# Grouping by array mode in a scan of two linear-attention mixers: sums on 64 rows into two PSUM banks, neighbours by sums over features

## The chip, the cores and the metric

The kernel runs on one core of a Trainium2 chip. The metric is the device time in microseconds (us) of one launch. The engines are PE (matrix products), DVE, ACT and POOL (elementwise work, each with its own in-order queue) and SP, which here only issues transfers.

## The reference

One layer of a backbone over 2048 latent tokens and 256 context tokens, of width 1024. After a modulated RMSNorm, one dense projection makes the inputs of two bidirectional linear-attention mixers of four heads each. The first, GLA, has a decay for each of 64 key features; the second, Gated DeltaNet (GDN below), has a short convolution, one decay per head and delta rules. Both scan over chunks forward and backward, and start the latent tokens from the context's final state. In GLA one chunk needs decayed scores, an output and a new state:

```python
bc = jnp.cumsum(gc, axis=3)
diff = bi[:, :, :, None, :] - bi[:, :, None, :, :]
dec = jnp.exp(jnp.where(causal[:, :, None], diff, -jnp.inf))
att = jnp.einsum('bhtd,bhsd,bhtsd->bhts', qi, ki, dec)
o = jnp.einsum('bhtd,bhde->bhte', qi * jnp.exp(bi), s) + jnp.einsum('bhts,bhse->bhte', att, vi)
s_new = s * jnp.exp(bl[:, :, 0, :])[..., None] + jnp.einsum('bhsd,bhse->bhde', ki * jnp.exp(bl - bi), vi)
```

The outputs of both directions are added, normalised per head, gated, projected (`w_gla_out`, `w_gdn_out`), merged by sigmoid gates, projected by `w_o` and added to the input, which a last RMSNorm normalises.

## The kernel before

It has three phases. `phase_proj` (to about 1375 us) makes all inputs in dense products and stores them in device memory; `phase_mix` (to about 1820) runs the scans; `phase_out` runs the output products. Chunks are of 128 tokens: 2 of context and 16 latent.

`phase_mix` is a loop of 17 steps, `si`. Step `si` prepares the chunk `si` of the forward direction and the chunk `15 - si` of the backward one (`gla_load`, `gla_step`) and, at the same time, scans the pair that the step before prepared (`gdn_scan` and `gla_scan`, one of each per direction). Each is a Python generator; `weave` takes a piece of each in turn, by weights, and a scheduler in the build then fixes one order for each engine. From there every queue is in order: an instruction that waits holds up all behind it.

Scores of GLA within a chunk are built by levels, `LEVELS = (64, 32, 16, 8, 4, 2, 1)`: at level m, the later block of each pair of blocks of m tokens looks at the earlier one. Per group of two levels (`gla_group`, three groups), PE sums the log decays over tokens, for 128 features at a time (`ct`) and both directions, in products with a table of zeros and ones, `wt` (L1110: 128 rows, 256 columns, type fp32r, the decays split into a high part `gh` and a low part `gl`). ACT takes the exponentials out of PSUM (L1192, L1195), DVE multiplies them by q (L1201) and POOL by k (L1202). `gla_lev` then makes one level's scores: four heads of 64 features, hence four products on 64 rows of PE (L1226), into one of two slots of the PSUM tile `lv`. A slot is copied into the scores `at` by ACT for m = 64 (two copies, L1230) or, with a mask, by DVE (L1233). Level 1, the neighbours, needs only each token's own decay: transposes (L1213), exponentials (L1215), a product with q (L1216), then `gla_lev` like the others.

`gla_ends` makes the decays to the chunk's ends (L1110, L1119), `gla_kt` and `gla_qe` the decayed keys and queries. `gla_scan` updates the state (L1282, products with 64 columns) and makes the outputs: scores times values (L1306, 128 rows), the queries times the state (L1310, 64 rows), written to `oi` by ACT (L1314) or, when the other direction's output `prev` exists, added to it by DVE (L1316). `gdn_scan` has blocks of four products with 128 rows at L1042, L1053, L1063, L1072 and L1082; its output is complete at L1083. A product in f32 is two passes on PE, so that a block of four shows as x8 in the trace.

For the first eight scanned pairs the outputs are only stored (`put_o`). After that each chunk's output meets the stored one of its other direction, loaded by `prev_o`, and goes through `finish`, four times a step: four squares on ACT with a sum (L1344), Ln and Exp on ACT (L1345, L1346), a normalisation on POOL (L1347), four transposes on PE (L1352), a gating product on DVE (L1354), with a load of the gates and a store of the result. The squares and their sums go to tiles with two buffers, so that a third finish waits for the normalisation of the first. I call these steps the second half of the mix, the others the first half. `finish` runs woven into the end of its step.

"Array mode" below is the shape of the part of PE that a product uses: 128 rows by 128 columns, 64 rows by 128 columns, 128 rows by 64 columns.

## Time and profile before

| | |
|---|---|
| time before, median of 3 runs | 2199.81 us (2198.74 to 2201.21) |
| the profiled execution: its time | 2198.7 us |
| its span | 2196.9 us |
| mean granted clock of PE | 0.989 |
| DMA traffic | 315.68 MB, 142 GB/s over the span |

A profile page gives the busy time of each engine, then the span in slices, DMA queues, the chain of work that ended last, and the costliest groups of instructions. A row of a timeline holds the start, the duration, the engine, the line of the kernel, the operation with output and inputs, the part of PE in use (rows*columns), the shape, the number of instructions joined in the row and, in brackets, the idle time of the engine just before and who ended it. A row of groups holds the sum of busy time, the mean in ns, and the idle time before. On PE durations overlap, since products are pipelined: the pace is the distance between starts.

### The profile page before, as it was taken

Reading aid. Unit: us, or ns where it says so; the run is one execution under the profiler, and the core shown is the slowest. Engines: PE = TensorE matmul, PEld = TensorE weight load, DVE = VectorE, ACT = ScalarE, POOL = GpSimd, SP = SyncE. Lnnn points to the kernel's source line nnn. Section 1 sums busy time; section 2 is a strip of 40 time slices with the busy share of each in tenths; the row PEclk is TensorE's granted clock in tenths of the full one; section 3 lists DMA queues with packets and bytes.
Section 4 is the critical chain, followed back from the end, with each engine's and each line's share of the span. In section 5 each row is a group of like instructions: output and inputs, shape, how many; then the busy total and the mean of one; then the engine's idle time right before and its main releaser. Section 6 shows DMA issues by size and latency. Waiting matters only on the chain. (4 is left out here: it accounts for less than half of the span.)

```text
span 2196.9 us, 40078 instructions
## 1 busy us (share of the span) xinstructions
PE 2122.3 (97%) x15168; PEld 1764.3 (80%) x15168; DVE 1245.2 (57%) x2178; ACT 884.2 (40%) x2188; POOL 858.2 (39%) x765
## 2 busy tenths in 40 slices
PE   5999999999999999999999998999999988999998
PEld 2688888888888888777777776888878877999888
DVE  3813555567776554655555554666777776444333
ACT  3654255455542223443434443444544444111211
POOL 2410122222320115665666662555555554322331
PEclk8999999999999999999999999999999999999999
DMA  8323122222222234443444435888688858433322
GB/s 281 104 89 115 53 60 68 63 63 61 70 75 74 83 89 137 140 141 116 134 150 145 146 134 174 281 303 277 227 267 287 263 176 254 138 120 125 101 80 84
DMA packets 275005, 315.68 MB, mean 144 GB/s; under 512 B 22280, under 2 KB 206716, under 8 KB 274812
## 3 DMA queue, kind: packets, MB, share of 16 engines
q1 hardware_dynamic: 274812, 313.12, 44.4%
q8 instruction: 120, 1.97, 0.4%
q14 instruction: 73, 0.60, 0.1%
HBM read 203.20 MB, written 109.84 MB: 142 GB/s over the span
## 5 line engine op out<-in xcount | busy, mean ns | idle before, releaser
L365 PE MATMUL pz<-hi,wh 128*128 128x512 f32 (+1 forms) x1560 | 621.3, 399 | 1.7 <-DVE hi L133 1.7
L365 PE MATMUL pz<-lo,wh 128*128 128x512 f32 (+1 forms) x1560 | 600.3, 385 | 1.8 <-POOL lo L134 1.8
L365 PE MATMUL pz<-hi,wl 128*128 128x512 f32 (+1 forms) x1520 | 588.0, 387 | 0.0
L365 PEld LDWEIGHTS pz<-lo,wh 128*128 128x128 f32 x1560 | 294.5, 189 | 51.0 <-POOL lo L134 3.6
L365 PEld LDWEIGHTS pz<-hi,wh 128*128 128x128 f32 x1560 | 294.2, 189 | 48.0 <-DVE hi L133 2.5
L365 PEld LDWEIGHTS pz<-hi,wl 128*128 128x128 f32 x1520 | 286.2, 188 | 53.7 <-issue 0.4
L134 POOL TENSOR_TENSOR wl<-w,wh 128x1024 fp32r<-128x1024 f32 x44 | 110.6, 2514 | 436.2 <-ACT wh L131 311.9
L563 DVE SCALAR_TENSOR_TENSOR acc<-zpad,cw,acc 128x1024 f32<-128x1024 f32 x192 | 268.2, 1397 | 6.7
L1519 PE MATMUL pm<-yh,wab 128*128 128x256 f32 x1024 | 187.9, 284 | 4.4 <-DVE mt L1523 4.4
L867 DVE CAST_PREDICATED U<-kit,pl 128x256 f16<-128x256 int32 x216 | 91.3, 432 | 138.7 <-PE pl L990 134.9
L1519 PEld LDWEIGHTS pm<-yh,wab 128*128 128x128 f32 x1024 | 161.3, 193 | 5.1 <-ACT wo L131 4.7
L1588 PE MATMUL pz<-wo,mh 128*128 128x512 f32 (+1 forms) x528 | 161.2, 388 | 0.0
L1519 PE MATMUL pm<-yl,wab 128*128 128x256 f32 x512 | 145.7, 285 | 0.8 <-POOL yl L134 0.8
L983 ACT CAST ppb<-pl 128x256 f16<-128x256 f32 x216 | 73.6, 374 | 166.4 <-PE pl L982 160.0
L1588 PEld LDWEIGHTS pz<-wo,mh 128*128 128x128 f32 x528 | 98.4, 189 | 20.2
L134 DVE TENSOR_TENSOR sql<-sq,sqh 128x512 fp32r<-128x512 f32 (+1 forms) x36 | 28.0, 805 | 141.6 <-ACT sqh L131 141.4
L618 POOL TENSOR_TENSOR acc<-acc,sq 128x512 f32<-128x512 f32 x32 | 50.2, 1576 | 138.4 <-ACT sq L617 78.6
L1588 PE MATMUL pz<-wo,ml 128*128 128x512 f32 (+1 forms) x264 | 101.8, 386 | 0.0
L1519 PEld LDWEIGHTS pm<-yl,wab 128*128 128x128 f32 x512 | 98.7, 193 | 1.7 <-POOL yl L134 1.2
L1202 POOL TENSOR_TENSOR E<-E,ak 128x256 f32<-128x256 f32 x96 | 76.8, 820 | 58.9 <-ACT E L1192 44.7
L134 POOL TENSOR_TENSOR yl<-wr,yh 128x1024 fp32r<-128x1024 f32 x16 | 40.3, 2542 | 134.2 <-ACT yh L131 134.2
L1233 DVE COPY_PREDICATED at<-am,lv 128x512 f32<-128x512 int32 x96 | 70.5, 734 | 31.5 <-PE lv L1226 29.4
(292 smaller groups left out, 4190.5 us busy)
## 6 DMA issues: line engine op xcount, KB each, us to landing
dgate<-ob SPq DMA_DIRECT2D x96, 256.0 KB
gd<-dgd SPq DMA_DIRECT2D x32, 768.0 KB
w<-in_w_in SPq DMA_DIRECT2D x44, 512.0 KB
qk<-dqkv SPq DMA_DIRECT2D x32, 512.0 KB
ga<-dgate SPq DMA_DIRECT2D x64, 256.0 KB
dqkv<-acc SPq DMA_DIRECT2D x192, 64.0 KB
dgd<-tm SPq DMA_DIRECT2D x36, 256.0 KB
dgd<-n SPq DMA_DIRECT2D x36, 256.0 KB
```

Source lines behind the costliest of these rows:

```text
L134: getattr(nc, lo).tensor_tensor(dst_lo, src, dst_hi.bitcast(F32), op=ALU.subtract)
L365: nc.tensor.matmul(ps[:, 0:n], a[:, kk, :], b[:, kk, :], start=(k == 0), stop=(k == last - 1))
L563: nc.vector.scalar_tensor_tensor(acc, src, wcol, acc, op0=ALU.mult, op1=ALU.add)
L618: nc.gpsimd.tensor_tensor(v, v, r, op=ALU.mult)
L867: self.nc.vector.copy_predicated(out, mv, data)
L983: nc.scalar.copy(ppl, pc.rearrange("p h (j i) -> p h j i", i=m))
L1202: nc.gpsimd.tensor_tensor(E[:, :, li, 1], E[:, :, li, 1], k, op=ALU.mult)
L1233: nc.vector.copy_predicated(at, self.am[:, i].unsqueeze(1).unsqueeze(1).broadcast_to([P, 2, 2, P]), ps)
L1519: nc.tensor.matmul(ps[:, half * 256:half * 256 + 256], wab[wi][:, k, j * P:(j + 1) * P], yy[:, k, :], start=(i == 0), stop=(i == 11))
L1588: nc.tensor.matmul(ps, aa[:, k, i * P:(i + 1) * P], wo[k][wi][:, cs], start=(j == 0), stop=(j == 23))
```

## The change

1. The table for the levels holds, for each half of a chunk's tokens, only that half's 64 columns (`WL` falls from 1024 to 640 columns a direction), since no level reaches over the middle of a chunk. A sum over tokens is made per half `x`: 64 rows of PE, 128 columns, into one PSUM bank for each half. A group has 16 such products, in pairs of the two halves, where it had 8 of full height. The exponentials are taken by half, eight a group.
2. Level 1 no longer goes through `gla_lev`. DVE makes decay times q of each token's neighbour, POOL multiplies by k (`gla_ones`), and two products with a two-column matrix `bones` sum over each head's 64 features (`gla_near`); a masked copy puts them into `at`.
3. `gla_lev` takes two levels at once: eight products on 64 rows, one after another, into both slots, and then the copies.
4. GLA's scan loses its own generator. `gla_state` makes both directions' new states in one block of 64-column products; `gla_out` makes both directions' outputs, the 64-row products last, right ahead of the first `gla_lev`. Both are called from the next pair's `gla_step`. The outputs of both directions go to one tile `og`, with one buffer, and the stored ones come in one tile `prevg`. The tiles `oi` and `prev` have two buffers where they had four.
5. The last step leaves out both mixers' state updates (`end`, `gla_end`).

The core of the diff. Lines that go are in the functions printed above.

```diff
-WL = 8 * P
+WL = 2 * P + 6 * 64
...
+            for x in range(2):
+                u = np.arange(64 * x, 64 * x + 64)
+                u = np.concatenate([u[np.isin(u, q)], u[~np.isin(u, q)]])
+                lev[i, 64 * x:64 * x + 64] = w[2 + i][64 * x:64 * x + 64][:, u]
+        cols = np.concatenate([*w[:2], *lev], 1)
...
-    def gdn_scan(self, r, need_o):
+    def gdn_scan(self, r, need_o, end=False):
...
-            oi = self.op.tile(B4, F32, name="oi", bufs=4)
+            oi = self.op.tile(B4, F32, name="oi")
...
+        if not end:
...
     def gla_group(self, r, i0):
...
+        E = self.gE.tile([P, 2, 2, 2, 2, 64], F32, name="E", bufs=3)
+        kl = self.gq.tile([P, 2, 2, P], F32, name="kl", bufs=3)
+        cols = slice(2 * P + i0 * 64, 2 * P + (i0 + 2) * 64)
+        ps = [self.pe().rearrange("p (l b c n) -> p l b c n", l=2, b=4, c=2) for _ in range(2)]
         for ct in range(2):
+            for d in range(2):
+                for j, g in enumerate(r["gg"]):
+                    for x in range(2):
+                        rows = slice(64 * x, 64 * x + 64)
+                        out = ps[x][:, :, 1:3, ct] if d == 0 else ps[x][:, :, 0:4:3, ct]
+                        nc.tensor.matmul(out, g[rows, d, ct * P:(ct + 1) * P], self.wt[rows, d, cols],
+                                         start=(j == 0), stop=(j == 1))
         for li in range(2):
+            m = LEVELS[i0 + li]
+            for x in range(2):
+                for qk in range(2):
+                    o = E[:, li, qk, x]
+                    if m == 64:
+                        i = ps[x][:, li, 1:3] if x != qk else ps[x][:, li, 0:4:3]
+                        i, o = i.rearrange("p a c n -> p c a n"), o.rearrange("p c (a n) -> p c a n", a=2)
+                    else:
+                        i = ps[x][:, li, 2 * qk:2 * qk + 2].rearrange("p e c (j i) -> p e (c j) i", i=m)
+                        o = o.rearrange("p c (j e i) -> p e (c j) i", e=2, i=m)
+                    nc.scalar.activation(o, i, AF.Exp, scale=1.0 / 16)
+        yield
+        for li in range(2):
+            nc.vector.tensor_tensor(E[:, li, 0], E[:, li, 0], byx(q), op=ALU.mult)
+            nc.gpsimd.tensor_tensor(byx(kl[:, li]), E[:, li, 1], byx(k), op=ALU.mult)
+        yield
+        return [(at, kl[:, li], E[:, li, 0], LEVELS[i0 + li]) for li in range(2)]
...
     def gla_ones(self, r):
...
+        w = self.gq.tile([P, 2, P], F32, name="qk1", bufs=1)
...
+        for d in range(2):
+            nc.vector.tensor_tensor(w[:, :, d:P:2], E[:, :, 1 - d:P:2], q[:, :, 1 - d:P:2], op=ALU.mult)
+        nc.gpsimd.tensor_tensor(w, w, k, op=ALU.mult)
+        return w
+    def gla_near(self, at, w):
+        nc = self.nc
+        pd = self.pe()
         for ct in range(2):
+            nc.tensor.matmul(pd[:, 2 * ct:2 * ct + 2], w[:, ct], self.bones, start=True, stop=True)
+        B = [P, 4, P]
+        nc.vector.copy_predicated(at, self.am[:, len(LEVELS) - 2].unsqueeze(1).broadcast_to(B),
+                                  pd[:, 0:4].unsqueeze(2).broadcast_to(B))
+    def gla_lev(self, levs):
+        nc, got = self.nc, []
+        for at, ks, ql, m in levs:
+            ps = self.slot()
+            for ct in range(2):
+                for hp in range(2):
+                    rows = slice(64 * hp, 64 * hp + 64)
+                    nc.tensor.matmul(ps[:, hp, ct], ks[rows, ct], ql[rows, :, ct], start=True, stop=True)
+            got.append((self.byhalf(at), ps, m))
+        for at, ps, m in got:
+            if m == 64:
+                for x in range(2):
+                    rows, cols = slice(64 * x, 64 * x + 64), slice(64 - 64 * x, 128 - 64 * x)
+                    nc.scalar.copy(at[rows, :, :, cols], ps[rows, :, :, cols])
+            else:
+                i = LEVELS.index(m) - 1
+                nc.vector.copy_predicated(at, self.am[:, i].unsqueeze(1).unsqueeze(1).broadcast_to([P, 2, 2, P]), ps)
+    def gla_step(self, f, b, prev):
...
+        if prev is not None:
+            S = self.gla_state(prev)
+            yield
+        levs = yield from self.gla_group(f, 0)
...
+        more = yield from self.gla_group(f, 2)
...
+        if prev is not None:
+            done = self.gla_out(prev, S)
+        self.gla_lev(levs)
+        if prev is not None:
+            done()
+            yield
+            yield from self.gla_put(prev)
+        yield
+        last = yield from self.gla_group(f, 4)
+        yield
+        self.gla_lev(more)
...
+        w = self.gla_ones(f)
...
+        yield
+        self.gla_lev(last)
+        yield
+        self.gla_near(f["at"], w)
+        yield
+    def gla_state(self, pair):
...
+        for d, r in enumerate(pair):
+            for h in range(4):
+                ct, hp = h // 2, h % 2
+                nc.tensor.matmul(ps[64 * hp:64 * hp + 64, (2 * d + ct) * P:(2 * d + ct + 1) * P],
+                                 r["kt"][:, 64 * h:64 * h + 64], r["v"][:, h * P:(h + 1) * P], start=True, stop=True)
...
+    def gla_out(self, pair, S):
...
+        po = [self.pv().rearrange("p (d c t) -> p d c t", d=2, c=2) for _ in range(2)]
...
+            nc.tensor.matmul(po[h % 2][:, 0, h // 2], f["at"][:, h], f["v"][:, h * P:(h + 1) * P],
+                             start=h < 2, stop=False, skip_group_check=True)
+        for d, r in enumerate(pair):
             for h in range(4):
...
+                nc.tensor.matmul(po[h % 2][:, d, ct], r["qe"][rows, ct], S[d][rows, ct], start=False,
+                                 stop=d == 1 and h >= 2, skip_group_check=True)
+        def done():
+            o = self.og = self.op.tile([P, 2, 4, P], F32, name="og", bufs=1)
+            v = lambda t, hp: t.rearrange("p d (c h) t -> p h d c t", h=2)[:, hp]
+            for hp in range(2):
+                if f["prev"] is None:
+                    nc.scalar.copy(v(o, hp), po[hp])
...
+                    nc.vector.tensor_tensor(v(o, hp), v(f["prev"], hp), po[hp], op=ALU.add)
+        return done
+    def gla_put(self, pair):
+        for d, r in enumerate(pair):
+            yield from self.put_o(0, r["c"] - NCTX, self.og[:, d])
...
+        t = pair[0]["prev"] = self.op.tile([P, 2, 4, P], F32, name="prevg", bufs=1)
+        for d, l in enumerate(ls):
+            self.nc.sync.dma_start(self.flat(t[:, d]), self.d_o[0][l])
...
+        t = self.op.tile([P, 4, P], F32, name="prev")
...
+                pair = [x[0] for x in prev]
+                self.gla_prev(pair)
+                for x in prev:
+                    x[1]["prev"] = self.prev_o(1, x[1]["c"] - NCTX)
+                for x in prev:
+                    gens.append((self.gdn_scan(x[1], True, si == len(order)), 12))
+                if si == len(order):
+                    gens.append((self.gla_end(pair), 4))
...
+                gens.append((self.gla_step(*[x[0] for x in cur], pair if si else None), 24))
```

What this does to PE's queue, in a step of the second half (`lv` is the PSUM tile of the levels, `pe` and `pz` are the other PSUM banks, `oi` an output that is being finished). Before:

```order
L1128 MATMUL pe<-kf,E_18553 128x128 x2
L1082 MATMUL pz<-vn,gd 128x128 x8
L1226 MATMUL lv<-ql,E 128x128 x4
...
L1226 MATMUL lv<-ql,E 128x128 x4
L1128 MATMUL pe<-kf,E_18654 128x128 x2
L1213 MATMUL pe<-kf,g_18495 128x128 x4
L1352 MATMUL pe<-kf,oi 128x128 x2
L1226 MATMUL lv<-ql,E 128x128 x4
L1352 MATMUL pe<-kf,oi 128x128 x8
L1226 MATMUL lv<-ql,E 128x128 x4
L1352 MATMUL pe<-kf,oi 128x128 x6
```

Four outputs are finished in a step: their sixteen transposes at L1352 come in three pieces, with one level of scores, four products on 64 rows at L1226, ahead of and between them. After, the same place:

```order
L1086 MATMUL pz<-vn,gd 128x128 x8
L1330 MATMUL pz<-av,at 128x128 x4
L1335 MATMUL pz<-Sa_19240,q_19167 128x128 x4
L1335 MATMUL pz<-Sa_19243,q_19173 128x128 x4
L1253 MATMUL lv<-E,kl 128x128 x8
...
L1201 MATMUL pe<-wt,gl_19602 128x2x2x32 x2
L1253 MATMUL lv<-E,kl 128x128 x8
L1132 MATMUL pe<-kf,E_19708 128x128 x2
L1229 MATMUL pe<-kf,g_19573 128x128 x4
L1045 MATMUL pz<-Sb_19760,qk 128x128 x4
L1045 MATMUL pz<-Sb_19768,qk 128x128
L1253 MATMUL lv<-E,kl 128x128 x8
L1241 MATMUL pe<-bones,qk_19874 128x2 x2
```

The outputs of both directions (L1330, L1335) now stand right ahead of the first two levels (L1253), whose eight products stand together; the next two follow eight pairs of sums, and the transposes at L1398 (L1352 before) all come behind the product with `bones`.

ACT's queue in the second half, from the exponentials or the copy of the decayed keys at the first half of a step to the last group's exponentials (`E<-pe`). Before:

```order
L1130 COPY akt<-pe 128x256
L1344 ACTIVATE fy,fss<-oi 128x128
L1345 ACTIVATE fss<-fss,cb 128x4
L1346 ACTIVATE fss<-fss 128x4
L1344 ACTIVATE fy,fss<-oi 128x128 x4
L1230 COPY at<-lv 64x2x2x64 x2
L1195 ACTIVATE E<-pe 128x2x16x4 x2
L1195 ACTIVATE E<-pe 128x2x32x2 x2
L1195 ACTIVATE E<-pe 128x2x16x4 x2
L1195 ACTIVATE E<-pe 128x2x32x2 x2
L1345 ACTIVATE fss<-fss,cb 128x4
L1130 COPY akt<-pe 128x256
```

Five squares at L1344 stand between the copy of the keys and the two copies of the 64-level; behind those the last group's exponentials follow at once. After:

```order
L1134 COPY akt<-pe 128x256
L1390 ACTIVATE fy,fss<-og 128x128 x2
L1390 ACTIVATE fy,fss<-oi 128x128
L1390 ACTIVATE fy,fss<-og 128x128 x2
L1259 COPY at<-lv 64x2x2x64 x2
L1391 ACTIVATE fss<-fss,cb 128x4
L1390 ACTIVATE fy,fss<-oi 128x128
L1392 ACTIVATE fss<-fss 128x4
L1390 ACTIVATE fy,fss<-oi 128x128 x3
L1391 ACTIVATE fss<-fss,cb 128x4
L1390 ACTIVATE fy,fss<-oi 128x128
L1392 ACTIVATE fss<-fss 128x4
L1390 ACTIVATE fy,fss<-oi 128x128 x2
```

Five squares (now L1390) stand ahead of the copies at L1259, and seven more, with two Ln and two Exp, between those copies and the eight exponentials at L1214.

More of the change, by code (lines that the diff above doesn't have):

```diff
@@ L1066, in gdn_scan @@
         yield
-        S2 = self.st.tile(B4, F32, name=f"Sb{d}")
-        if S is not None:
-            nc.gpsimd.tensor_tensor(S2, S, self.bc(self.egl, c, d), op=ALU.mult)
-        ps = self.heads(self.pv())
-        for h in range(4):
-            nc.tensor.matmul(ps[:, h], r["kt"][:, h], vn[:, h], start=True, stop=True)
-        if S is None:
-            nc.vector.tensor_copy(S2, ps)
-        else:
-            nc.vector.tensor_tensor(S2, S2, ps, op=ALU.add)
-        self.Sb[d] = S2
-        yield
+        if not end:
+            S2 = self.st.tile(B4, F32, name=f"Sb{d}")
+            if S is not None:
+                nc.gpsimd.tensor_tensor(S2, S, self.bc(self.egl, c, d), op=ALU.mult)
+            ps = self.heads(self.pv())
+            for h in range(4):
+                nc.tensor.matmul(ps[:, h], r["kt"][:, h], vn[:, h], start=True, stop=True)
+            if S is None:
+                nc.vector.tensor_copy(S2, ps)
+            else:
+                nc.vector.tensor_tensor(S2, S2, ps, op=ALU.add)
+            self.Sb[d] = S2
+            yield
         if need_o:
@@ L1168, in ctx_loads, with gla_ctx_states @@
         return [[(self.gla0[d, d ^ i], gdn[d, d ^ i]) for d in range(2)] for i in range(2)], rest
+    def gla_ctx_states(self, pairs):
+        for p in pairs:
+            self.gla_state([x[0] for x in p])
+            yield
+            yield
     def gla_ctx(self, pairs):
@@ L1220, in gla_lev @@
         nc = self.nc
-        ps = self.slot()
-        at = self.byhalf(at)
+        pd = self.pe()
         for ct in range(2):
-            for hp in range(2):
-                rows = slice(64 * hp, 64 * hp + 64)
-                nc.tensor.matmul(ps[:, hp, ct], ks[ct][rows], ql[rows, ct], start=True, stop=True)
-        if m == 64:
-            for x in range(2):
-                rows, cols = slice(64 * x, 64 * x + 64), slice(64 - 64 * x, 128 - 64 * x)
-                nc.scalar.copy(at[rows, :, :, cols], ps[rows, :, :, cols])
-        else:
-            i = LEVELS.index(m) - 1
-            nc.vector.copy_predicated(at, self.am[:, i].unsqueeze(1).unsqueeze(1).broadcast_to([P, 2, 2, P]), ps)
@@ L1312, in gla_scan @@
-            for x, y, hs in parts:
-                if prev is None:
-                    nc.scalar.copy(x, y)
-                else:
-                    nc.vector.tensor_tensor(x, self.byhalf(prev)[:, hs], y, op=ALU.add)
-            yield
-            yield from self.put_o(0, l, o)
+                nc.tensor.matmul(po[h % 2][:, d, ct], r["qe"][rows, ct], S[d][rows, ct], start=False,
[6 more added lines that the diff above has]
+                    nc.scalar.copy(v(o, hp), po[hp])
+                else:
+                    nc.vector.tensor_tensor(v(o, hp), v(f["prev"], hp), po[hp], op=ALU.add)
@@ new lines, in gla_out, with gla_end, gla_prev @@
+        return done
+    def gla_put(self, pair):
+        for d, r in enumerate(pair):
+            yield from self.put_o(0, r["c"] - NCTX, self.og[:, d])
+    def gla_end(self, pair):
+        self.gla_out(pair, self.Sa)()
+        yield
+        yield from self.gla_put(pair)
+    def gla_prev(self, pair):
+        ls = [r["c"] - NCTX for r in pair]
+        if ls[0] not in self.seen[0]:
+            pair[0]["prev"] = None
+            return
+        t = pair[0]["prev"] = self.op.tile([P, 2, 4, P], F32, name="prevg", bufs=1)
+        for d, l in enumerate(ls):
+            self.nc.sync.dma_start(self.flat(t[:, d]), self.d_o[0][l])
@@ L1322, in prev_o @@
             return None
-        t = self.op.tile([P, 4, P], F32, name="prev", bufs=4)
+        t = self.op.tile([P, 4, P], F32, name="prev")
         self.nc.sync.dma_start(t.rearrange("p h t -> p (h t)"), self.d_o[i][l])
@@ L1383, in phase_mix @@
         mp = self.pool("mix", 1, ctx=gctx)
+        self.bones = mp.tile([P, 2], F32, name="bones")
+        for x in range(2):
+            nc.vector.memset(self.bones[64 * x:64 * x + 64, x:x + 1], 1.0)
+            nc.vector.memset(self.bones[64 * x:64 * x + 64, 1 - x:2 - x], 0.0)
         self.am = mp.tile([P, len(LEVELS) - 1, P], I32, name="am")
@@ L1419, in phase_mix @@
                     gens.append((itertools.chain(*[self.gdn_scan(p[d][1], False) for p in pairs]), 8))
-                    gens.append((itertools.chain(*[self.gla_scan(p[d][0], False) for p in pairs]), 4))
+                gens.append((self.gla_ctx_states(pairs), 4))
             else:
-                for i in range(2):
-                    for x in prev:
-                        x[i]["prev"] = self.prev_o(i, x[i]["c"] - NCTX)
-                for (a, b) in prev:
-                    gens.append((self.gdn_scan(b, True), 12))
-                    gens.append((self.gla_scan(a, True), 8))
+                pair = [x[0] for x in prev]
[6 more added lines that the diff above has]
+                    gens.append((self.gla_end(pair), 4))
             cur = []
```

102 lines of the change are left out of this document (18 added, 84 removed).

## The prediction, made before the changed kernel ran

> **What bounds the kernel now.** I read the page's busy times first, then the busy times of two stretches (one step of the mix each, the first from the half whose outputs are only stored, the second from the half whose outputs meet their other direction), then PE's timeline, and last the timeline of all engines and the groups by shape.
>
> ```profile
> PE 2122.3 (97%) x15168; PEld 1764.3 (80%) x15168; DVE 1245.2 (57%) x2178; ACT 884.2 (40%) x2188; POOL 858.2 (39%) x765
> ```
>
> ```profile
> core 0: us, PE busy (x) PEld busy (x) DVE busy (x) ACT busy (x) POOL busy (x), PEclk, DMA share, GB/s
> 1532.30:1556.60 24.30, 23.54 (x218) 20.94 (x217) 17.08 (x31) 11.66 (x47) 13.08 (x15) 1.00 0.72 236
> 1692.90:1721.40 28.50, 26.56 (x235) 22.96 (x234) 20.90 (x47) 14.35 (x74) 17.01 (x19) 1.00 0.84 274
> ```
>
> PE is the bound: it idles 24.30 - 23.54 = 0.76 us in a first-half step and 28.50 - 26.56 = 1.94 in a second-half step, at full clock. So only two things count: what PE has to do, and what it waits for. What it does is paced by weight loads and by changes of array mode:
>
> ```profile
> 1531.38 1.05 PE L1063 MATMUL pz<-rhs,gd 128*128 128x128 f32 x8
> 1532.27 1.11 PE L1306 MATMUL pz<-av,at 128*128 128x128 f32 x8
> ...
> 1533.31 0.71 PE L1310 MATMUL pz<-Sa,q 64*128 64x128 f32 x8
> 1533.95 1.16 PE L1063 MATMUL pz<-rhs,gd 128*128 128x128 f32 x8
> 1535.04 0.72 PE L1310 MATMUL lv<-Sa,q 64*128 64x128 f32 x8
> ...
> 1535.91 0.28 PE L1110 MATMUL pe<-wt,gl 128*128 128x256 f32 x1
> 1536.03 0.28 PE L1110 MATMUL pe<-wt,gh 128*128 128x256 f32 x1
> ...
> 1547.19 0.72 PE L1226 MATMUL lv<-ql,E 64*128 64x128 f32 x8 [0.76 <-DVE at L1233]
> ```
>
> By starts, the block of four 128-row products at L1063 takes 1532.27 - 1531.38 = 0.89 beside its own kind, and 1535.04 - 1533.95 = 1.09 between two 64-row blocks. Going to 64 rows and back thus costs 0.20; the 64-row block of L1310 takes 1533.95 - 1533.31 = 0.64 where its eight 64-row passes, two side by side at 0.112 (eight full passes take 0.89), need 0.45: 0.19 more. One change of mode costs about 0.196. A sum at L1110 starts every 0.12.
>
> **First half, eight steps.** Counted in the order of one step, the mode changes fall from 20 to 12: 8 x 0.196 = 1.57 off. The 24 sums of a step (three groups of eight) become 24 pairs of 64-row sums. No row shows a 64-row sum; the nearest is the 64-row pass of L1310 at 0.056, so 24 x 0.112 = 2.69 against 24 x 0.12 = 2.88: 0.19 off. (Bounds: nothing saved, or 24 x 0.06 = 1.4 if a half-width sum also streams in half the time.) The neighbours' block of 64 rows (0.45) becomes two products with two columns, whose nearest row is
>
> ```profile
> 932.68 0.50 PE L899 MATMUL pe<-bones,R 128*128 128x2 f32 x4
> ```
>
> four passes, so 0.45 to 0.50: no difference. DVE's work stays about equal; POOL gets one product more a step (L1234), priced below by L1202's 0.82, off PE's path in this half. PE's own work: -1.75.
>
> Against that, a pair of levels now fills both slots of `lv` at once, so the second pair can only begin when the first is evacuated, and the outputs' copies stand ahead of that on ACT. Rows for these:
>
> ```profile
> L1314 ACT COPY oi<-lv 128x512 f32<-128x512 f32 x8 | 4.7, 587 | 8.0 <-PE lv L1310 8.0
> ```
>
> ```profile
> L1316 DVE TENSOR_TENSOR oi<-prev,lv 128x512 f32<-128x512 f32 x7 | 4.8, 681 | 0.0
> L1201 DVE TENSOR_TENSOR ql<-E,q 128x256 f32<-128x256 f32 x94 | 66.8, 745 | 22.5 <-ACT E L1195 21.6 <-ACT E L1192 0.5
> ```
>
> ```profile
> L1202 POOL TENSOR_TENSOR E<-E,ak 128x256 f32<-128x256 f32 x94 | 75.2, 820 | 58.7 <-ACT E L1192 44.5 <-ACT E L1195 14.1
> L1347 POOL TENSOR_TENSOR oi<-oi,fss 128x512 f32<-128x512 f32 x28 | 31.7, 1131 | 1.3 <-ACT fss L1346 1.3
> ```
>
> ```profile
> 1729.74 0.30 ACT L1345 ACTIVATE fss<-fss,cb 128x4 f32<-128x4 f32 x1
> 1730.07 0.20 ACT L1346 ACTIVATE fss<-fss 128x4 f32<-128x4 f32 x1
> 1730.20 1.27 DVE L1083 TENSOR_TENSOR oi<-pz,oi 128x512 f32<-128x512 f32 x2
> ...
> 1730.97 0.31 ACT L1344 ACTIVATE fy<-oi 128x128 f32<-128x128 f32 x1 [0.70 <-DVE oi L1083]
> 1731.28 0.29 ACT L1344 ACTIVATE fy<-oi 128x128 f32<-128x128 f32 x1
> ...
> 1732.16 0.73 ACT L1230 COPY at<-lv 64x256 f32<-64x256 f32 x2
> ...
> 1732.91 1.48 ACT L1195 ACTIVATE E<-pe 128x128 f32<-128x128 f32 x8
> ...
> 1733.03 0.72 PE L1226 MATMUL lv<-ql,E 64*128 64x128 f32 x8 [1.02 <-ACT at L1230]
> ...
> 1734.24 0.73 DVE L1233 COPY_PREDICATED at<-am,lv 128x512 f32<-128x512 int32 x1
> ...
> 1737.11 0.44 PE L1352 MATMUL pe<-kf,oi 128*128 128x128 f32 x2 [0.47 <-POOL oi L1347]
> ...
> 1737.46 1.03 SPq L1340 DMA_DIRECT2D fg<-dgate  x2
> ...
> 1738.81 0.66 PE L1352 MATMUL pe<-kf,oi 128*128 128x128 f32 x4 [0.25 <-POOL oi L1347]
> ```
>
> From the end of the outputs at L1335: two copies of 512 elements 1.17, two copies of the 64-level 0.73, the masked copy of the 32-level 0.73, hand-overs 0.5, together 3.1. PE has in that time two levels (0.9), eight pairs of sums (0.9) and a change (0.2): 2.0. New wait at L1253: about 1.2, where 0.76 goes. (Between 0, if the copies run side by side with the masked copy, and 2.) Net: -1.75 + 1.2 - 0.76 = -1.3 a step, times 8 = -10.5.
>
> **Second half, seven steps.** Mode changes fall from 22 to 12: -1.96, with the sums -2.15. But all four outputs of a step are now ready only after L1086 and L1335, at one moment, where today GLA's two come half a step earlier (L1306, L1310). ACT is in order, and each finish starts with four squares of 0.30 (1731.28 - 1730.97). In ACT's new order five squares stand ahead of the 64-level's copies and seven more, with two Ln and two Exp, ahead of the last group's exponentials. Today's row at 1733.03 shows what squares ahead of those copies do: PE waits 1.02. Four waits follow:
>
> 1. L1253, second pair of levels: sum into `og` 0.68, five squares 1.5, copies 0.73, masked copy 0.73, hand-over 0.3: 3.9 against PE's 2.0. About 2.0.
> 2. L1229, whose PSUM bank the last exponentials free: from the end of the 64-level's copies ACT has seven squares 2.1, two Ln and Exp 1.0, eight exponentials 1.48: 4.6. PE has a masked copy to wait for (0.73 + 0.1, part of wait 1), two levels and a change 1.1, a transposed pair 0.22: 2.2. About 2.4, and 1.1 more where the third finish's squares need the tile that POOL's normalisation still reads.
> 3. L1253, last pair: POOL's two products 1.64 and a hand-over 0.2 against PE's transposes and five state products, 1.2. About 0.6.
> 4. L1241 waits for POOL's product at L1234, behind two normalisations of 1.13: 2.26 + 0.82 = 3.1 from the end of POOL's other products, against one pair of levels, 1.1: 2.0, or 0.9 if one normalisation has gone before. I take 1.5.
>
> Together 6.5 where 1.94 stood: -2.15 + 6.5 - 1.94 = +2.4 a step, times 7 = +17. The waits' bounds are 1.94 (the squares find gaps; ACT is busy only 14.35 of 28.50) and about 9 (6.5, 1.1 for the tile, 0.5 more at wait 4 and 1.1 at wait 3 where a normalisation stands ahead of the products).
>
> GLA's finishes take their transfers along on SP's queue: two loads of gates issue in 1.03 us (row at 1737.46), so four in some 2, and they are read at L1400 after squares, Ln, Exp, a normalisation and transposes; nothing, or 1 us a step if the stores of `og` are queued ahead of them.
>
> **The edges.** The last state updates of both mixers are left out: two blocks of eight 128-row passes, 0.89 each, and one block of eight with 64 columns, no longer: 2.7 at most. Against it GLA's last outputs and their two finishes end later, eight squares or 2.4. Net 0, from -3 to +5. The shorter table of weights, loaded and copied long before the mix, is hidden by the projections' PE work; if it were not, it would be a gain. The single buffer of the stored outputs is read at the end of one step and loaded for the end of the next, a step of over 20 us to cover a load.
>
> Sum: -10.5 + 17 + 0 = +6.5 on the profiled execution of 2198.7, which lies 1.1 under the median: 2199.81 + 6.5 = 2206.
>
> **The rivals.** *Faster: the squares slide into ACT's gaps.* For it: ACT is half idle, and what holds PE is queue order alone. If a second-half step keeps its 1.94 of waits, -10.5 - 15 = -25.5 gives 2174; with waits half-way, 4.0, it is -11 and 2189. It decides at waits of 5.6, where both halves cancel. Against it: the squares' source appears late whatever ACT does, and the row at 1733.03 already shows the wait with four of them. Chance 0.28.
>
> *No change.* Waits of 5 to 6.2 give -4 to +4, 2196 to 2204: fewer mode changes, paid back exactly by the finish. This takes wait 2 without the stall for a tile, and wait 4 at its lower end. Chance 0.2.
>
> *Much slower: the change doesn't give side-by-side sums.* If two 64-row sums do not share the array (different banks, a half-width stream), each costs a full load, 0.112 as a pass of the row at 932.68 (0.50 for four, pipelined): 48 x 0.112 = 5.4 in place of 2.69, +2.7 a step. In the first half all of it shows, +21; in the second PE then waits less, +7: 2234. Against it: L1310's rows, 64 rows in two banks at 0.056. Chance 0.06.
>
> [...]
>
> **How the numbers follow.** The finish chain as costed (waits over 6.2) has 0.46, with the rival of the sums 0.52 slower; 0.2 is within 0.2%, 4.4 us, about what a measurement of this kernel can tell; 0.28 is faster. The range goes down to waits of 3 (-10.5 - 7.6 = -18, 2182), leaving out the fullest gain, and up to waits of 9 (-10.5 + 34 = +24, 2223) and most of the way to the rival of the sums, 2230. The likeliest case's own range is 2204 to 2223.
>
> **What would show it.** Right: first-half steps of about 23.0, second-half steps near 31, with PE's waits at L1253 for ACT at L1259, at L1229 for ACT at L1214 and at L1241 for POOL at L1234, and sums starting every 0.056. Wrong: second-half steps under 28.5; PE waiting there for nothing of ACT's; pairs of sums at 0.2; or a mode change that costs PE nothing, so that first-half steps stay at 24.3 without a wait.

## The result, and the profile after

The changed kernel takes 2227.8 us (median of 4 executions, 2220.02 to 2230.58) against 2199.93 before: 1.012 of the time, with a 95% interval of 1.0098 to 1.0143. It is slower, by 28 us, where 6 were forecast. The profiled execution took 2220.02 us, its span 2218.2, 21.3 more than before; it is the fastest of the four, and the comparison below is made with it.

The busy times and the clock of the page after (the slices of the clock are tenths of full speed, 55 us each):

```profile
PE 2109.8 (95%) x15456; PEld 1770.2 (80%) x15456; DVE 1223.5 (55%) x2180; ACT 883.7 (40%) x2212; POOL 866.8 (39%) x779
...
PEclk9999999999999999999999999999989889999999
```

PE is busy for 12.5 us less, and waits for 34 us more. From about 1600 us on, in the second half of the mix, its clock no longer stands at full speed, as it did before. The busy times of a step of each half show both (first the half whose outputs are stored, then the half whose outputs meet):

```profile
core 0: us, PE busy (x) PEld busy (x) DVE busy (x) ACT busy (x) POOL busy (x), PEclk, DMA share, GB/s
1529.70:1553.00 23.30, 21.84 (x238) 20.23 (x237) 14.79 (x32) 11.53 (x48) 13.69 (x16) 1.00 0.77 244
1668.50:1700.30 31.80, 26.28 (x254) 23.80 (x253) 20.71 (x47) 14.61 (x76) 18.49 (x21) 0.89 0.87 288
```

The first half falls by 1.0 a step: PE's work from 23.54 to 21.84, its idle time from 0.76 up to 1.46. The second half rises by 3.3, from 28.50 to 31.80, and its row has a clock of 0.89. Where that comes from shows in three windows of that step, one behind the other:

```profile
1678.43:1681.84 3.41, 1.23 (x24) 1.11 (x22) 1.22 (x2) 3.37 (x20) 0.49 (x1) 1.00 1.03 414
1681.84:1688.67 6.83, 5.49 (x33) 4.64 (x32) 3.52 (x9) 5.46 (x34) 4.93 (x6) 0.50 0.86 308
1688.67:1692.08 3.41, 3.29 (x37) 3.09 (x36) 2.41 (x5) 0.62 (x1) 2.98 (x4) 1.00 0.37 97
```

In 3.41 us PE was busy for 1.23; then the granted clock is 0.50 for 6.83 us, twice as long; then it is full again. The same stands at 1617, 1648, 1743 and 1774 in that profile (1.23 to 1.34 busy, then 0.50 for 6.83), always on one grid of 3.41 us. In the kernel before the emptiest window of the seven second-half steps on its grid is this one, 2.16 of 3.41 (the emptiest of the whole mix, at 1392.70, has 2.08), and the clock stays full behind it:

```profile
1703.30:1706.71 3.41, 2.16 (x20) 1.53 (x19) 1.33 (x3) 3.37 (x21) 2.85 (x5) 1.00 0.95 388
1706.71:1710.12 3.41, 2.86 (x26) 1.98 (x26) 2.96 (x6) 1.79 (x11) 3.41 (x4) 1.00 0.61 189
```

On this grid the granted clock is 1.00 or 0.50 in every window of both profiles, and from 1360 to 2200 us it stands at 0.50 for 3.41, 6.83 or 10.24 us at a time (after: from 1862.74, 1681.84 and 1715.97). The window ahead of the halving shown is not an idle one: PE is busy for 36% of it.

So a second-half step divides into work at full clock, idle time, and what the halved clock adds. Busy 26.28, of it 5.49 at a clock of 0.50: half of that, 2.74, I put down to the clock, which leaves 23.54 work and 5.52 idle. It is an estimate; pairs of sums start every 0.21 at half clock (from 1603.14) and every 0.11 at full. Before: 26.56 work, 1.94 idle. Hence -3.0 by work, +3.6 by waits, +2.7 by the clock, +3.3 in all. The waits of PE from 1610 to 1830, by the waiting line and who ended it:

```profile
PE lv L1253 <- DVE at L1262: 15.3, 7, 2.2
PE pe L1229 <- ACT E L1214: 11.9, 7, 2.2
PE pe L1114 <- DVE fy L1400: 6.2, 5, 1.8
...
PE pe L1241 <- POOL qk L1234: 0.3, 1, 0.3
```

The first two are the forecast's chain, which ACT's timeline shows: five squares, the copies, seven squares with a stall for POOL's normalisation, and only then the exponentials that PE waits for at 1717.02. DVE's masked copy, for which PE waits at 1713.29, starts when ACT's copies end.

```profile
1710.17 0.31 ACT L1390 ACTIVATE fy<-og 128x128 f32<-128x128 f32 x1 [4.17 <-DVE og L1345]
...
1711.36 0.30 ACT L1390 ACTIVATE fy<-og 128x128 f32<-128x128 f32 x1
...
1711.65 0.73 ACT L1259 COPY at<-lv 64x256 f32<-64x256 f32 x2
...
1714.24 0.31 ACT L1390 ACTIVATE fy<-oi 128x128 f32<-128x128 f32 x1 [0.56 <-POOL og L1393]
...
1715.83 1.48 ACT L1214 ACTIVATE E<-pe 128x128 f32<-128x128 f32 x8
```

```profile
1712.42 0.73 DVE L1262 COPY_PREDICATED at<-am,lv 128x512 f32<-128x512 int32 x1 [1.68 <-ACT at L1259]
```

```profile
1713.29 1.16 PE L1253 MATMUL lv<-E,kl 64*128 64x128 f32 x16 [2.19 <-DVE at L1262]
1714.38 0.44 PE L1132 MATMUL pe<-kf,E 128*128 128x128 f32 x2
1717.02 1.12 PE L1229 MATMUL pe<-kf,g 128*128 128x128 f32 x4 [2.20 <-ACT E L1214]
1717.93 2.34 PE L1045 MATMUL pz<-Sb,qk 128*128 128x128 f32 x10
1720.20 2.08 PE L1253 MATMUL lv<-E,kl 64*128 64x128 f32 x16
```

2.19 and 2.20 us of idleness lie within six. Behind them ten passes at L1045 take 2.34 and two levels 2.08; at full clock, in a first-half step, they take 1.28 and 1.16. That step also shows pairs of 64-row sums starting every 0.11 and the first half's wait at L1253:

```profile
1539.91 0.28 PE L1201 MATMUL pe<-wt,gl 64*128 64x128 f32 x2
1540.02 0.28 PE L1201 MATMUL pe<-wt,gh 64*128 64x128 f32 x2
...
1541.37 1.16 PE L1253 MATMUL lv<-E,kl 64*128 64x128 f32 x16 [0.96 <-DVE at L1262]
...
1543.18 1.28 PE L1045 MATMUL pz<-Sb,qk 128*128 128x128 f32 x10
1544.39 1.16 PE L1253 MATMUL lv<-E,kl 64*128 64x128 f32 x16
```

A ledger of the 21.3 us, by the first product of L1063 (now L1066) in each step, after less before: up to the second step +3.8 (1409.6 against 1405.8), over the next seven -7.5, at the step in which stored outputs are first loaded +4.7, over the next seven +17.5, and +2.7 in the output phase. The seven rise by 2.5 each on average and not by 3.3: the first of them only by 1.5 and the last by 0.1.

### The profile page after: what moved, and what is told of

The parts are those of the page before. It is cut to its first block, busy times and chain, and to the rows that moved or that the text cites. A ratio compares the mean times of both kernels' runs of the same rounds, so it can differ in the third digit from the quotient of the medians.

```text
span 2218.2 us, 40515 instructions
## 1 busy us (share of the span) xinstructions
PE 2109.8 (95%) x15456; PEld 1770.2 (80%) x15456; DVE 1223.5 (55%) x2180; ACT 883.7 (40%) x2212; POOL 866.8 (39%) x779
## 5 line engine op out<-in xcount | busy, mean ns | idle before, releaser
L1218 POOL TENSOR_TENSOR kl<-E,ak 128x256 f32<-128x256 f32 x96 | 79.3, 845 | 64.7 <-ACT E L1214 64.7
L1217 DVE TENSOR_TENSOR E<-E,q 128x256 f32<-128x256 f32 x96 | 55.0, 579 | 68.7 <-ACT E L1214 45.4
```

What stands on the lines that cost most here:

```text
L1217: nc.vector.tensor_tensor(E[:, li, 0], E[:, li, 0], byx(q), op=ALU.mult)
L1218: nc.gpsimd.tensor_tensor(byx(kl[:, li]), E[:, li, 1], byx(k), op=ALU.mult)
```

## The experiments

Theory A: waits for ACT's queue, in which the squares stand ahead of copies and exponentials, leave PE idle for over 3 us in six, and that halves the clock. Rivals are named with each run. Ratios are to the kernel before on the same chip.

**Filling the waits, twice.** Products of the identity with itself, which nothing reads:

```diff
+        pt = self.pe()
+        n = 8 if prev is not None and prev[0]["prev"] is not None else 0
+        self.fill(pt, n)
         self.gla_lev(more)
         yield
+        self.fill(pt, n)
-        self.gla_kt(b)
+        self.gla_kt(b, pt)
```

> The changed kernel, with work added that nothing reads: in each of the seven second-half steps, two blocks of eight products of the identity with itself (1.79 us by the pace of 0.224 for one), one ahead of the second pair of levels and one ahead of the decayed keys' transposes, where the changed kernel's PE waits 2.19 and 1.0 to 2.2 us. Theory A (the waits for ACT's finish chain leave PE busy in less than about half of a window of 3.41 us, after which the granted clock is halved for 6.8 us): the clock stays full in those steps, each falls from 31.2 to 32.4 us to 29 to 30, and the whole falls by 10 to 20 us, to 2208 to 2218, although PE has 25 us more to do. Rival B (only the waits themselves cost, the clock's reading does not matter): the added work fits into the waits or lengthens them, 2227 to 2235. Rival C (the clock is lowered because PE is busier with 64-row products, by load and not by idleness): more load, 2230 and above.

2240.43 us, 1.017 [1.0151, 1.0189]. A's number missed. The filled waits came back behind the filling, 1.66 at the last pair of levels and 0.6 to 1.1 at the neighbours' sums, so that in the 3.41 us from 1660.70 PE was busy for 1.58, 46%. The clock was halved as before (0.90 over the first step below). The second filling has `self.fill(pt, n and 7)` and `self.fill(pt, n and 3)` at those two places:

> The kernel of the first filling (two blocks of eight products that nothing reads in each second-half step) with two more, where that kernel's PE still waited: seven products (1.57 us) ahead of the last pair of levels, where it waited 1.66, and three (0.67) ahead of the neighbours' sums, where it waited 0.7 to 0.9. PE's work at full clock rises from 27.4 to 29.6 us a step. Theory A (idle PE halves the clock, and the halved clock lengthens the step): idle falls to under 1.5 us a step, no window under half is left, the clock stays full, and the steps fall from 34.0 to 31 or 31.5: with more to do, 15 to 21 us faster than the first filling, 2219 to 2226. Rival G (the halved clock only fills time in which PE would have waited for ACT, DVE and POOL anyway): steps stay at 34 or grow, 2238 to 2256.

2240.82 us, 1.0183 [1.0161, 1.0206]. A step of the first filling, then one of the second:

```profile
1643.40:1677.40 34.00, 30.53 (x287) 28.36 (x286) 21.91 (x47) 14.65 (x78) 17.82 (x20) 0.90 0.70 231
```

```profile
1682.10:1715.90 33.80, 30.24 (x306) 27.91 (x305) 21.71 (x47) 14.11 (x75) 17.21 (x20) 1.00 0.74 258
```

The clock is now full in this step, and in four of the seven: the waits at the last pair of levels, up to 1.7, are 0.2 at most, and those at the neighbours' sums are gone. But the step isn't shorter. PE has 2.2 us more to do and idles 3.56, of which 1.9 is a wait that the filling itself brought (it writes to the bank that ACT copies the keys from). By A's number this fails, and by G's it stands: what the full clock gave, the added work and waits took. That the halved clock costs its full 2.7 us a step is not shown by this pair. That more load lowers the clock (rival C) is refuted: with the most work of all, 30.24 in this step, it was 1.00.

**No squares.**

```diff
-        for h in range(4):
-            nc.scalar.activation(sq[:, h], src[:, h], AF.Square, accum_out=ss[:, h:h + 1])
+        nc.gpsimd.memset(ss, 1.0)
```

> The changed kernel with the sixteen squares of a step's finishes left out (the sums are set to one by POOL, so that the outputs aren't normalised by their own size). Theory A and rival B agree that ACT's queue makes the waits ahead of the second pair of levels and of the transposed decays: both shrink, to under 1 us each. A: with them go the windows under half and the halved clock in the second half, second-half steps of 25 to 26.5 us, 2227.8 - 7 x 6 = 2180 to 2192. B: only the waits' 3.5 us a step go, 2200 to 2206. If neither wait shrinks (the late outputs themselves are what is waited for, not the squares), 2220 to 2230.

2199.22 us, 0.9997 [0.9984, 1.0009]: 28.6 off, a little below B's range, short of A's. So what the change lost comes back when the squares go. The wait at the transposed decays all but went (1.7 in all). The one ahead of the second levels stayed at up to 2.4, for POOL: the memset stands ahead of its products with k, a cost of the edit. The clock was still halved in five of the seven steps, so this run doesn't part the waits' price from the clock's. Two steps, with and without a halved clock:

```profile
1666.80:1694.70 27.90, 25.02 (x255) 23.13 (x254) 21.03 (x47) 10.20 (x45) 17.95 (x25) 0.94 0.93 316
1694.70:1723.00 28.30, 23.85 (x255) 21.77 (x254) 21.08 (x47) 10.50 (x47) 18.51 (x25) 1.00 0.89 274
```

The step with 3.41 us at half speed is not the longer one: it idles 2.88 where the other idles 4.45. Here a short halving did not lengthen the step.

**GLA's outputs early**: `self.gla_out(prev, S)()` and the stores moved right behind `gla_state`.

> The changed kernel with GLA's outputs taken right behind the state update, ahead of the step's first group of sums, in place of right ahead of the first levels; so their eight squares come in the first third of the step, as in the kernel before. One more pair of mode changes, 0.4 us a step. Theory A: the waits at the second pair of levels and at the transposed decays fall to 1 us or less, no window under half, second-half steps of 25.5 to 27.5 and first-half steps of 23 to 23.7, in all 2175 to 2195, below the kernel before. Rival B (no clock): 2200 to 2208. If the grouping itself is what costs, 2220 or more.

2252.14 us, 1.0233 [1.0218, 1.0248], 57 above A's range; by the number alone it is the third case. First-half steps fall to 23.10, with 0.7 idle. But in the second half the squares now stand ahead of the first groups' exponentials: PE waits 1.8 to 2.0 for those (L1201) and 2.0 to 2.6 at L1327 for the state's update on DVE, the clock is halved for 10 to 18 us a step (0.85 over the one of 35.30 from 1653.90), and steps take 34.7 to 38.7. The place of the squares changed which wait they make, not that they make one.

**The scan as before**, with its own generator and buffers; only sums, pairs of levels and neighbours are new.

> One part of the change alone: sums by halves into two banks, levels in pairs and neighbours by features, but GLA's scan as in the kernel before, with its own generator, outputs per direction and buffers, and the last state updates kept. Theory A: the outputs' place is what costs, so this kernel has short waits and a full clock in the second half: first-half steps of 23.3 to 24, second-half steps of 26.5 to 28.5, 2180 to 2198. Rival D (pairs of levels in both slots cost the time, whatever the outputs do): waits ahead of the second pair of over 2 us in the second half, windows under half, 2210 to 2230.

2224.18 us, 1.0109 [1.0094, 1.0124]. This is rival D's number: without the outputs' move nearly all of the loss is there. Second-half steps take 31 to 33, the last 36, with a wait like this one in each (2.1 to 2.3), and in six of the seven 3.41 or 6.83 us at half clock beside it:

```profile
1695.11 1.72 PE L1253 MATMUL lv<-E,kl 64*128 64x128 f32 x16 [2.32 <-DVE at L1262]
```

Ahead of the 64-level's copies ACT has six squares and a Ln here. The kernel before had four there and waited 1.02 for one slot; a pair needs both, so that the masked copy comes on top. That this is the reason is not shown, and the next run speaks against it. The loss is also made up otherwise than the changed kernel's:

```profile
1679.30:1710.50 31.20, 27.86 (x253) 24.66 (x253) 21.09 (x48) 14.99 (x76) 17.11 (x21) 0.95 0.82 281
```

3.41 us of this step are at half clock, so by the same estimate 1.7 are the clock's, 26.1 work and 3.3 idle. Against the kernel before that is -0.4, +1.7 and +1.4. The changed kernel's step has 2.6 less work than this one, and 3.2 more of waits and half clock: the outputs' move saves nearly as much as it loses.

**Single levels again**: each `gla_lev` call with one level.

> The changed kernel with levels one by one again, each in its slot, so that a level waits for one evacuated slot and not for two; the rest stays, the mode changes of a step rise by 6 to 8 (1.2 to 1.6 us). Theory A': the pairs are half of the wait; ahead of the third level PE waits about 1.2 in place of 2.2, and fewer windows fall under half: second-half steps of 29 to 31, first-half steps of 24, in all 2212 to 2225. Rival F (pairs cost nothing, since the second slot's copy runs while PE does the first level): only the mode changes are added, 2238 to 2250.

2247.05 us, 1.0205 [1.018, 1.0229]: F's number. The wait ahead of the third level fell to 1.55, with 0.36 more ahead of the fourth, together hardly less than the pair's 2.19. At the transposed decays PE waits 2.6, and the clock was halved in every second-half step (0.90 over the one from 1686.80). A first-half step:

```profile
1539.70:1564.60 24.90, 22.47 (x238) 20.40 (x237) 15.08 (x32) 11.63 (x48) 13.57 (x16) 1.00 0.69 226
```

Against 21.84 of 23.30, work is up by 0.63 and idleness by 0.97. Pairs gain in the second half too, where steps take 34.3 to 35.6 here, but for the last, and 31.2 to 32.4 with pairs. So, with the outputs late, it isn't the pairs that make the loss. Which part of the run before does is open: single levels with the scan as before were not run.

**All squares late**: a zero that ACT writes behind the last exponentials is the squares' bias. The tile `oi` gets four buffers as well.

```diff
+        nc.scalar.activation(self.late, E[:, 0, 0:1], AF.Copy, scale=0.0)
...
-            nc.scalar.activation(sq[:, h], src[:, h], AF.Square, accum_out=ss[:, h:h + 1])
+            nc.scalar.activation(sq[:, h], src[:, h], AF.Square, bias=self.late, accum_out=ss[:, h:h + 1])
```

> The changed kernel with the finishes' sixteen squares held back, by a bias that ACT writes (as zero) right behind the step's last exponentials, so that ACT's queue holds the copies of the 64-level and all exponentials first and the squares between two steps; the outputs have enough buffers for it. Theory A (squares ahead of the copies and the exponentials make the waits, and the waits then halve the clock): the wait ahead of the second pair of levels falls from 2.2 to the 1.0 of the first half, the one at the transposed decays goes, no window under half; second-half steps of 25.5 to 28, in all 2180 to 2200. Rival E (the second half is bound by the sum of ACT's, DVE's and POOL's work in a chain, wherever the squares stand): the squares, some 6 us in a row, hold up the next step's first exponentials instead, steps of 30 or more, 2218 or more.

2222.77 us, 1.0092 [1.0068, 1.0116]. The two waits are gone as A says (0.85, and none at L1229), the time isn't: rival E. PE now waits 0.6 to 1.3 at each finish's transposes for POOL, and for the next step's exponentials. This run has what the others lack, neighbouring steps with a full clock and with 6.83 us of half clock while PE was busy throughout:

```profile
1672.80:1706.00 33.20, 28.08 (x253) 25.47 (x253) 20.95 (x47) 16.58 (x77) 17.80 (x21) 0.90 0.84 265
1706.00:1735.40 29.40, 24.91 (x253) 22.43 (x253) 20.80 (x47) 16.45 (x77) 17.78 (x21) 1.00 0.81 259
```

The same 253 products take 3.17 more, and the step 3.8 more. In this pair of steps the halving cost all of itself. The step behind them, with 3.41 us at half clock, took 29.87, only 0.5 more than the one at full clock, though by the estimate 1.7 are lost there.

**A wait put into the kernel before**: the copies of the 64-level twice, and four times, in second-half steps (`for x in list(range(2)) * 2`, then `* 4`).

> The kernel before, with the two copies of the 64-level done twice in each second-half step: 0.73 us more on ACT at the place for which PE waits 1.02 today. Without the clock: 0.73 more of waiting in each of seven steps, 5 us, 2205; less if it is hidden. With theory A (a window of 3.41 us in which PE is busy less than about 0.56 halves the clock; the lowest windows of the kernel before in the mix are at 0.62): some steps fall under it and lose 1.7 to 3.4 us more, 2205 to 2220, with the granted clock at half somewhere between 1610 and 1810.

> The kernel before, with the same copies done four times: 2.2 us more on ACT at that place. Without the clock: 2.2 a step at most, seven steps, 15 us, 2215. With theory A: nearly every second-half step has a window under 0.56, and each loses 1.7 to 3.4 us beside, 2227 to 2239, by more than three times what the kernel with 0.73 us loses.

2207.22 (1.0036 [1.0023, 1.0049]) and 2213.26 (1.0062 [1.0046, 1.0078]): 8 and 14 us more. Of the 7.7 and 13.3 by which the profiled spans are longer, 6.7 and 7.4 lie in the seven steps, the rest outside them. PE's wait behind the copies, 0.9 to 1.6 in the kernel before, became 1.2 to 1.7 and 1.6 to 2.2, less than the added 0.73 and 2.2, so a single wait of 3 us was not put to the test. The jump that A expected isn't there: the clock was halved at two second-half places in each run (1623 and 1811; 1623 and 1712), 3.41 us each, and the mean clock is 0.990 in both profiles. Two windows of the second run, each with the one behind it:

```profile
1678.16:1681.57 3.41, 1.58 (x15) 1.39 (x12) 1.13 (x4) 3.24 (x14) 1.02 (x2) 1.00 0.95 365
1681.57:1684.98 3.41, 2.94 (x27) 2.22 (x28) 2.11 (x4) 3.39 (x21) 1.89 (x3) 1.00 0.56 208
1708.82:1712.23 3.41, 1.63 (x15) 1.14 (x15) 1.56 (x6) 3.29 (x16) 1.17 (x2) 1.00 0.87 325
1712.23:1715.64 3.41, 3.41 (x20) 2.85 (x20) 3.17 (x6) 2.87 (x15) 3.41 (x5) 0.50 0.38 101
```

The emptier one, 46% busy, leaves the clock full, the other, 48%, halves it: PE's busy share alone doesn't decide. One wait of up to 2.2 us a step seldom halved the clock; the changed kernel has two, close together. A's account of how little it takes was wrong.

**GLA's squares late, the other mixer's first.** The bias only for `mi == 0`, and:

```diff
-            self.fin.append((self.finish(i, l, o), 3))
+            self.fin.insert(0 if i else len(self.fin), (self.finish(i, l, o), 3))
```

> The changed kernel with the squares of GLA's two finishes held back behind the step's last exponentials, and the delta-rule mixer's two finishes first, so that their eight squares run while PE makes GLA's outputs. Ahead of the copies of the 64-level ACT has eight squares that start earlier, ahead of the exponentials none. Theory A: the wait ahead of the second pair of levels falls to about 1.6, the one at the transposed decays goes, fewer windows fall under half, second-half steps of 26 to 28.5, in all 2185 to 2205. Rival E (four finishes at once bind the step wherever they stand): steps of 30 or more, 2215 or more.

2203.5 us, 1.002 [1.0009, 1.003]: 24 of the 28 us are back, by the place of eight squares a step and the order of the finishes. Three of the seven steps, in a row, all at full clock:

```profile
1639.10:1666.30 27.20, 23.81 (x255) 21.84 (x254) 20.69 (x46) 15.78 (x79) 17.88 (x20) 1.00 0.86 286
1666.30:1694.60 28.30, 23.74 (x255) 21.75 (x254) 21.57 (x49) 15.79 (x78) 17.83 (x20) 1.00 0.94 312
1694.60:1721.40 26.80, 23.68 (x254) 21.75 (x253) 20.54 (x45) 15.69 (x78) 17.86 (x20) 1.00 0.88 285
```

PE's work is the changed kernel's, 23.7 against 23.54; idleness is 3.1 to 4.6 against 5.52, and the clock's 2.7 are gone. What is left is the wait ahead of the second pair:

```profile
1707.23 1.16 PE L1255 MATMUL lv<-E,kl 64*128 64x128 f32 x16 [1.94 <-DVE at L1264]
```

**A third buffer for the decays**: `bufs=3` for the tile `g`, on top of that.

> The kernel with GLA's squares held back, and a third buffer for the decays `g`, so that their load goes out a step earlier and no longer stands behind the stored outputs' loads on SP's queue. It tells what that load costs at the step where outputs first meet (PE waits 3.9 there, and 10 us at half clock follow), and in each first-half step (0.5 to 0.6 at the sums' second group). If the load is what the wait is for: 4 to 9 us off at that step, 0.5 in each of seven, 2191 to 2198, below the kernel before. If the stored outputs themselves are waited for, or the DMA engines are full: no change, 2202 to 2206.

2198.75 us, 1.0002 [0.9988, 1.0017]. The step in which stored outputs are first loaded takes 23.2 where it took 29.3 in the changed kernel, at full clock. The first-half steps hardly gain: the wait for the sums' second group is gone, but a second one of 0.66 comes ahead of the levels. And the second step of the mix waits 5.2 for POOL, where it waited 2.9 for a load in the run before, and takes 2.9 more.

```profile
1582.70:1605.90 23.20, 21.59 (x238) 20.07 (x237) 17.29 (x40) 9.84 (x41) 13.74 (x16) 1.00 0.85 285
```

So at that step the load of `g` was the wait. This version equals the kernel before and doesn't beat it.

**Four squares ahead of the copies, four behind**, in the version just shown: GLA's eight squares stay late, and of the other mixer's eight the second four get a zero as bias that ACT writes behind a level's copy. The order of the other mixer's two finishes is turned round with it.

```diff
+                nc.scalar.activation(self.mid, at[:, 0, 0, 0:1], AF.Copy, scale=0.0)
...
-            nc.scalar.activation(sq[:, h], src[:, h], AF.Square, bias=0.0 if mi else self.late,
+            nc.scalar.activation(sq[:, h], src[:, h], AF.Square, bias=self.late if not mi else self.mid if hold else 0.0,
```

> As the run before, and the squares of the delta-rule mixer's second finish are held until the 64-level's copies are made, so that four squares stand ahead of the copies and four, with Ln and Exp, ahead of the last exponentials. Theory A: the wait ahead of the second pair of levels falls from 1.9 to about 0.8, some 0.3 to 0.8 appears at the transposed decays; 0.3 to 0.8 us a step less, 2 to 6 us under the run before. If the finishes bind the step as a chain: no change or slower.

2213.53 us, 1.0071 [1.0058, 1.0085]: a miss. The wait ahead of the second levels fell to 1.08 as expected, but up to 1.58 came back at the transposed decays and up to 1.57 at the last levels: in this kernel four squares ahead of the last exponentials cost more than ahead of the copies.

## Why the prediction was right and where it fell short

- **The array modes and sums.** Forecast -1.75 of work in a first-half step; measured 23.54 to 21.84, -1.70. Pairs of 64-row sums start every 0.11, so the rival of sums at twice the price is out. Their weight loads start every 0.11 as well (rows of PEld from 1539.51). That loads set PE's pace fits the rows before, where sums of 256 columns start every 0.12, passes of 128 columns every 0.112, and four of two columns take 0.50: the pace hardly follows the columns, and each has one load. In the second half the mode changes fell from 22 to 12, as counted, but work by 3.0 where 2.15 were forecast; where the other 0.85 comes from is open.
- **The first half's new wait.** Forecast 1.2 at L1253, measured 0.96. Unforeseen was 0.45 to 0.6 at L1201 for the exponentials at L1123, which stand behind the late load of `g`. So -1.0 a step, not -1.3.
- **The finish chain.** Wait 1 was put at 2.0 and is 2.19; wait 2 at 2.4 and is 1.0 to 2.2. Both are shown to be the squares' place: with all squares late they are 0.85 and none. Waits 3 and 4 (2.1) did not come: 0.3 in all at L1241. In their place PE waits 0.7 to 1.8 at L1114 in five of the seven steps, for a bank that the gating product at L1400 still reads. Together 5.5 in the step shown, where 6.5 stood.
- **The clock.** It is in no term of the sum: "at full clock" was read from before and kept for after. The halved clock adds 2.7 us of PE time, by the estimate, in the second-half step shown. How much of the 2.7 would otherwise have been idle time, such as the absent waits 3 and 4, stays open: a halving cost 3.8 us in one kernel's step and nothing in another's. The times spread with it: the changed kernel's four executions took 2220.0 at a mean clock of 0.977, 2226.8 and 2228.8 at 0.973, and 2230.6 at 0.971. Why the clock differs between them was not shown.
- **Luck.** The seven second-half steps rose by 17.5 where 17 were forecast, but term by term the forecast is off: 0.85 more saved, 1.0 less waited, and 2.7 by the clock, which stood at nothing. That makes +3.3 for a step where +2.4 was forecast, and the first and the last of the seven, which rose by 1.5 and 0.1, bring the seven back to 17.5. The result, 2227.8, also lies above the 2204 to 2223 of the likeliest case. It is within 2230 because the range had been drawn out for the rival of the sums, which didn't come.
- **The edges.** "Net 0, from -3 to +5" is the term that was most mis-sized. The second step waits 2.6 for the load of the values and then runs 6.83 us at half clock; the first step with stored outputs waits 3.78 for `g`, whose load SP issues behind the loads of outputs that have only just been stored; the output phase adds 2.7. About 11 in all, most of what lies between the forecast's 6.5 and the profile's 21.3; the first half gave 7.5 in seven steps where 10.5 stood for eight. The single early sentence on `prevg`, that a load has over 20 us, overlooked what is queued behind it on SP.
- **Which part.** The forecast put the loss down to the outputs' move. The run with the scan as before, 2224, loses nearly as much without it, by less waiting and half clock and by less saved work. What the sums by halves, the pairs of levels and the neighbours' sums each bring there is not shown; single levels made it worse, not better.

## What to carry to other kernels

When a change saves work on the engine that binds, look at what its in-order neighbours have queued ahead of the next thing it needs: work of 3.0 us a step was saved in the second half, and more than that was lost to waits behind sixteen squares and to the halved clock that came with them. Moving eight of them, with the order of the finishes, gave back 24 us without touching PE's work. Where PE's waits would come close together, lay the windows of 3.41 us on which this clock changed over them: in the changed kernel it was the idle time within such a window that went with a halved clock. The wait of 2.19 ahead of 1713.29 lies for 1.45 us in the window from 1709.15, behind which the clock stayed full, and for 0.73 in the next one, which holds 1.15 of the second wait too; behind that one it was 0.50.

## What the runs showed of the hardware

- A change of array mode costs 0.196 us by the rows before (L1063 and L1310 from 1531.38 to 1535.04), and with it the step's work at full clock followed to within 0.05 in the first half: -1.75 forecast, -1.70 measured.
- In the changed kernel's mix, from 1380 to 1830, the clock was 0.50 behind each of the ten windows of 3.41 us at full clock in which PE was busy for 55% or less (the fullest 1.88, at 1398.53), and stayed at 1.00 behind all with 57% or more (the emptiest 1.96, at 1709.15). Elsewhere the line isn't as sharp: in the same kernel's output phase the clock stayed full behind a window of 50% (1.71, at 1866.16), and with the copies done four times behind one of 46% (1.58, at 1678.16), while it was halved behind one of 48% (1.63, at 1708.82).
- In the changed kernel's mix a halving lasts 6.83 us, or 10.24 (from 1715.97 and 1811.54); in its output phase one lasts 3.41 (from 1862.74). A row on PE takes about 1.8 times as long in it: 1.16 to 2.08 for two levels, 1.28 to 2.34 for ten passes.
